# Two-layer encoder trunk in split fp32: the ring of split weights lies 64 bytes further along SBUF

## The chip, the cores and the metric

One core of a Trainium2 chip runs the whole program. The metric is the device time of one execution in microseconds (us), the median of several runs. TensorE (PE, with its weight loads shown apart as PEld), VectorE (DVE), ScalarE (ACT) and GpSimd (POOL) work from SBUF, 128 partitions wide; matmuls write to PSUM; SyncE (SP) issues the DMAs.

## The reference

Two requests of 256 tokens each, 1024 wide, pass through the same two layers. Each layer is a half-step SwiGLU block, a token mixer, another half-step SwiGLU block and a norm:

```python
def swiglu(x, w_gate, w_up, w_down):
    return (jax.nn.silu(x @ w_gate) * (x @ w_up)) @ w_down
...
    for layer in range(DEPTH):
        x = x + 0.5 * swiglu(rms_norm(x, ffn1_norm[layer]), ffn1_w_gate[layer], ffn1_w_up[layer], ffn1_w_down[layer])
        h = rms_norm(x, mix_norm[layer])
...
        x = x + 0.5 * swiglu(rms_norm(x, ffn2_norm[layer]), ffn2_w_gate[layer], ffn2_w_up[layer], ffn2_w_down[layer])
        x = rms_norm(x, final_norm[layer])
```

`D_FF` is 2816. The mixer of layer 0 joins differential attention with neighbourhood attention, that of layer 1 is grouped-query attention with rotary positions; each has one input and one output projection. All is float32.

## The kernel before

**Split operands.** Every float32 operand `a` of a large product is cut into a high part (an fp32r copy) and a low part (the rest, fp32r too), and a product is made of three matmuls: high by high, high by low, low by high. So each piece of weights is loaded by DMA into `raw`, copied by ACT into a tile `wh` (L349, `emit_hi`), and DVE (at times POOL) subtracts to give `wl` (L364, `emit_lo`). `wh` and `wl` are the ring of split weights: 12 tiles of 128 x 512 each (`RING`, L31), 2048 bytes of a partition apiece, reused in turn through the whole program.

**The two SwiGLU blocks of a layer** (`ffn`, L854) take nearly all the time. Gate and up are one product over 22 slices of `D_FF`. For the first two or three slices it is done plainly (`plain`, L957): the weights are the stationary operand and 512 tokens stream past, from the split tokens `xh`, `xl`. For the other slices seven products of blocks stand in for eight (`multiply`, L893, in `product_of`, L906): 128 x 128 weights stationary, 256 tokens streaming, from `xh`, `xl` or from sums of token blocks in `xb`. They go into the banks `ba`, `bb`, `bc`, `bg`. Groups of 4, 6, 6 and 6 slices (`GROUPS`, L22) are followed by the down product (`down`, L1033): weights stationary, 512 columns of the split activations `ah`, `al` streaming. In the last block of all, the last two rows of output go by 256 columns (`down_last`, L1067).

**The mixers.** The input projection (`in_proj_group`, L1248) has it the other way round: tokens `xh`, `xl` are stationary and 256 columns of `wh`, `wl` stream past into `ip`. The output projection (`out_proj`, L1266) is again weights stationary, with 512 columns of `mh`, `ml`, into `op`. Between them lie small matmuls of attention: `sc`, `pt`, `pv`.

**What sets the order.** The order of all instructions is fixed when the program is built: by a planner (`Plan`, L438) and an interleaver (`Interleave`, L1187) that reckon with costs of their own. Neither looks at where a tile lies within its row beyond blocks of 128 elements.

**Where tiles lie.** Pools are laid one behind the other along the partition: `per`, `sm`, `rawp`, `wp`, and then a pool of the stage (`ffn`, `ab` or `cc`). `per` holds the residual `X`, the tokens `xh`, `xl` and the sums `xb`. `sm` holds small tiles of 32 bytes, and one of 256 bytes, `rh` (L810), of which 16 bytes are used. `rawp` holds the two buffers of `raw`, `wp` the ring and the sums of weights `T1` to `T4`. The stage's pool holds `ah`, `al`, `gate`, `dt`, `mh`, `ml` and so on. The tiles of 1 KB and more start, in the program as built, at these bytes of the partition:

| tile | first byte before | past a multiple of 256, before | after |
|---|---|---|---|
| `xh`, `xl` | 33792, 50176 | 0 | 0 |
| `xb` (two) | 69120, 81408 | 0 | 0 |
| `sq`, `sum0`, `X` | 66560, 93696, 17408 | 0 | 0 |
| `sum1` (also `dg`) | 95776 | 32 | 32 |
| `raw` (two) | 100160, 108352 | 64 | 128 |
| ring `wh`, `wl` (24) | 116544 to 163648 | 64 | 128 |
| `T1` to `T4`, `dt`, `gate`, `ah`, `al`, `mh`, `ml` | from 165696 | 64 | 128 |
| `qkh`, `qkl`, `T`, `V` of the first mixer | from 208768 | 128 | 192 |

A weight block within a ring tile starts at a multiple of 512 bytes from the tile's start, a token block at a multiple of 1024, so the table holds for each block as for its tile.

Of the kernel before, what the change touches and what calls it, by code (L numbers as in the profile page):

```python
# [9 lines left out]
F32R = mybir.dt.float32r  # L10
# [5 lines left out]
P = 128  # L16
# [526 lines left out]
def hybrid_trunk_kernel(ctx, tc, x, cst, wgu1, wd1, wgu2, wd2, win_ab, wout_ab, win_c, wout_c, ali, nab, y):  # L543
# [8 lines left out]
    sm = ctx.enter_context(tc.tile_pool(name="sm", bufs=4))  # L552
# [17 lines left out]
    def pvp(name):  # L570
        return clock.alloc(pv_p.tile([P, T], F32, tag="pv", name=name), "pv", BANKS["pv"])

    def small(w, name):
        return sm.tile([P, 8], F32, tag=name, name=name)[:, :w]
# [76 lines left out]
    class Norm:  # L651
# [152 lines left out]
        def spread_steps(self, name, pool, tag):  # L804

            d = {}

            def high():
                d["v"] = getattr(self, name)
                rh = sm.tile([P, 64], F32R, tag="rh", name="rh", bufs=1)[:, :4]  # L810
                A.activation(rh, d["v"], AF.Copy)
                d["h"] = rh.bitcast(F32)

            def low():
                d["l"] = small(4, "rt")
                V.tensor_tensor(d["l"], d["v"], d["h"], ALU.subtract)

            def diagonal(v, tag):
                dg = per.tile([P, 4, P], F32R, tag=tag, name="dg")
                V.tensor_tensor(dg, ident.unsqueeze(1).to_broadcast([P, 4, P]),  # L820
                                d[v].unsqueeze(2).to_broadcast([P, 4, P]), ALU.mult)
                d[tag] = dg

            def spread():
                d["ps"] = pvp("bc")
                for i, tag in enumerate(("sq", "sum1")):
                    PE.matmul(d["ps"], lhsT=ones_r, rhs=d[tag].rearrange("p a b -> p (a b)"), start=(i == 0),
                              stop=(i == 1))

            def copy():  # L830
                self.wide[name] = out = pool.tile([P, T], F32, tag=tag, name=tag, bufs=1)
                V.tensor_copy(out, d["ps"])

            self.wide = getattr(self, "wide", {})
            return [("act", high, [name], ["rh"], 0.1), ("dve", low, [name, "rh"], ["rl"], 0.08),
                    ("dve", lambda: diagonal("h", "sq"), ["rh"], ["sq"], 0.61),
                    ("dve", lambda: diagonal("l", "sum1"), ["rl"], ["sum1"], 0.61),
                    ("pe", spread, ["sq", "sum1"], ["pv"], 0.5), ("dve", copy, ["pv"], [tag], 0.6)]
# [1062 lines left out]
```

## Time and profile before

| | |
|---|---|
| median of 3 runs | 1824.51 us (1820.37 to 1824.85) |
| the profiled execution: its time | 1817.23 us |
| its span, first to last instruction | 1815.5 us |
| mean granted TensorE clock | 0.996 |
| instructions in the span | 31467 |
| DMA | 175.53 MB, mean 97 GB/s |

The profile is of one execution. Busy time is the time in which an engine has at least one instruction under way. A matmul's record is longer than the time until the next one starts, since matmuls are pipelined. So a stretch of W us, in which x records are seen, has one matmul started every (W + length of one record) / x; this is called the pitch below. A name such as `ba<-xh,wh` gives the tile that is written and those that are read; buffer numbers are left out. Nearly all instructions carry line 151, the helper that records them, so tiles tell them apart, not lines.

### The profile page before, as it was taken

To read this page: it belongs to the slowest core of one execution; us is meant where nothing else is said; L and a number is where in the kernel's file an instruction comes from. 1 tells how busy PE (TensorE), PEld (TensorE's weight loads), DVE (VectorE), ACT (ScalarE), POOL (GpSimd) and SP (SyncE) were. 2 spreads that over 40 slices of the span, in tenths; PEclk is the share of its full clock that TensorE was granted. 3 is DMA by queue.
4 is the path that set the end of the run, shared out by engine and by line. 5 is a ranking of instruction groups with operands and counts; after the bars stand their busy time and mean duration, and the time that the engine had idled before them with its cause. 6 is when DMAs were issued, how large, how long until landed. Compare 5 with 4: busy or idle time off the path is not lost.

```text
span 1815.5 us, 31467 instructions
## 1 busy us (share of the span) xinstructions
PE 1772.1 (98%) x12428; PEld 1616.8 (89%) x12428; DVE 1517.2 (84%) x2849; ACT 959.4 (53%) x1975; POOL 155.9 (9%) x110
## 2 busy tenths in 40 slices
PE   8999999999899999999999999999998999999997
PEld 7998989898798889898978999999986788989896
DVE  8998979757886899898899989898777788989895
ACT  7463636445555646363665545455355664636362
POOL 0000000043431000000000000000344100000000
PEclk9999999999999999999999999999999999999999
DMA  4332323222212134141412232323121113324231
GB/s 153 119 129 91 119 91 120 105 94 71 82 71 94 47 117 141 69 145 67 142 67 93 96 117 97 113 99 132 53 71 47 68 39 128 129 82 136 74 117 47
DMA packets 31700, 175.53 MB, mean 97 GB/s; under 512 B 3392, under 2 KB 5696, under 8 KB 17088
## 3 DMA queue, kind: packets, MB, share of 16 engines
q1 hardware_dynamic: 31552, 173.52, 27.9%
q8 instruction: 97, 1.59, 0.4%
q14 instruction: 51, 0.42, 0.1%
HBM read 171.41 MB, written 2.10 MB: 96 GB/s over the span
## 4 chain that ended last, share of the span: by engine, by line
PE 78%; DVE 12%; ACT 5%; issue 2%; DMA 1%; POOL 1%; SPq 0%; POOLq 0%; ACTq 0%; DVEq 0%
PE ba L151 30%; PE bb L151 13%; PE bc L151 12%; PE bg L151 11%; PE ip L151 6%; PE op L151 4%; DVE wl L151 2%; ACT att L151 2%; DVE att L151 1%; PE pv L151 1%; DVE X L151 1%; DVE nm L151 1%; DVE dt L151 1%; DMA raw<-wd 1%; DVE xl L151 1%
## 5 line engine op out<-in xcount | busy, mean ns | idle before, releaser
L151 ACT ACTIVATE wh<-raw 128x512 fp32r<-128x512 f32 x553 | 337.8, 626 | 218.5 <-PE ba L151 63.2
L151 DVE TENSOR_TENSOR wl<-raw,wh 128x512 fp32r<-128x512 f32 x516 | 371.1, 727 | 59.4 <-ACT wh L151 53.5
L151 ACT ACTIVATE wh<-T 128x512 fp32r<-128x512 f32 x316 | 197.0, 629 | 262.5 <-PE ba L151 138.7
L151 PE MATMUL bc<-xb,wh 128*128 128x256 f32 x1264 | 225.7, 278 | 3.7 <-DVE us L151 3.2
L151 DVE TENSOR_TENSOR wl<-T,wh 128x512 fp32r<-128x512 f32 x316 | 215.2, 685 | 15.9 <-ACT wh L151 13.9
L151 PE MATMUL ba<-xh,wh 128*128 128x256 f32 (+1 forms) x704 | 204.7, 291 | 3.8 <-ACT wh L151 3.8
L151 PE MATMUL ba<-al,wh 128*128 128x512 f32 (+1 forms) x534 | 206.0, 386 | 0.0
L151 PE MATMUL ba<-ah,wh 128*128 128x512 f32 (+1 forms) x534 | 205.9, 386 | 0.0
L151 PE MATMUL ba<-ah,wl 128*128 128x512 f32 (+1 forms) x534 | 205.9, 386 | 0.0
L151 PE MATMUL ba<-xh,wl 128*128 128x256 f32 (+1 forms) x704 | 204.6, 291 | 0.0
L151 PE MATMUL ba<-xl,wh 128*128 128x256 f32 (+1 forms) x704 | 204.4, 290 | 0.0
L151 PEld LDWEIGHTS bc<-xb,wh 128*128 128x128 f32 x1264 | 191.0, 188 | 5.1 <-DVE us L151 3.6
L151 PE MATMUL bc<-xb,wl 128*128 128x256 f32 x632 | 175.2, 277 | 0.0
L151 PE MATMUL ip<-wh,xh 128*128 128x256 f32 x576 | 166.0, 288 | 0.0
L151 PE MATMUL ip<-wh,xl 128*128 128x256 f32 x576 | 160.7, 279 | 0.6 <-DVE xl L151 0.6
L151 PE MATMUL ip<-wl,xh 128*128 128x256 f32 x576 | 160.5, 279 | 0.0
L151 PEld LDWEIGHTS ba<-xh,wh 128*128 128x128 f32 x704 | 133.1, 189 | 7.8 <-ACT wh L151 4.0
L151 PEld LDWEIGHTS ba<-xh,wl 128*128 128x128 f32 x704 | 132.8, 189 | 3.9 <-DVE wl L151 0.5
L151 PEld LDWEIGHTS ba<-xl,wh 128*128 128x128 f32 x704 | 132.7, 189 | 3.4
L151 PEld LDWEIGHTS bc<-xb,wl 128*128 128x128 f32 x632 | 118.8, 188 | 0.0
L151 PEld LDWEIGHTS ba<-ah,wl 128*128 128x128 f32 x534 | 100.3, 188 | 20.1
L151 PEld LDWEIGHTS ba<-al,wh 128*128 128x128 f32 x534 | 100.3, 188 | 19.8 <-DVE al L151 0.2
(204 smaller groups left out, 4364.0 us busy)
## 6 DMA issues: line engine op xcount, KB each, us to landing
raw<-wgu SPq DMA_DIRECT2D x87, 1024.0 KB, 4.7
raw<-wd SPq DMA_DIRECT2D x48, 768.0 KB, 4.1
raw<-win_ab SPq DMA_DIRECT2D x12, 1024.0 KB, 4.7
raw<-wd SPq DMA_DIRECT2D x16, 512.0 KB, 3.6
raw<-win_c SPq DMA_DIRECT2D x6, 1024.0 KB, 4.8
raw<-wout_ab SPq DMA_DIRECT2D x4, 1024.0 KB, 4.8
raw<-wout_c SPq DMA_DIRECT2D x4, 1024.0 KB, 4.7
X<-x SPq DMA_DIRECT2D x8, 256.0 KB, 5.1
```

Source lines behind the costliest of these rows:

```text
L151: return f(*args, **kw)
```

## The change

The tile `rh` is made 80 elements wide in place of 64, 320 bytes in place of 256. Its used part stays four elements. What lies in front of it stays where it is; what lies behind it in the partition, the rest of `sm`, `raw`, the ring and the pools of the stages, starts 64 bytes later. On each of the five engines the program has the same instructions in the same order as before, on the same tiles.

```diff
             def high():
                 d["v"] = getattr(self, name)
-                rh = sm.tile([P, 64], F32R, tag="rh", name="rh", bufs=1)[:, :4]
+                rh = sm.tile([P, 80], F32R, tag="rh", name="rh", bufs=1)[:, :4]
                 A.activation(rh, d["v"], AF.Copy)
                 d["h"] = rh.bitcast(F32)
```

So the pairs that a matmul reads, streaming operand and stationary operand, lie like this (bytes past a multiple of 256):

| matmuls | streaming, before / after | stationary, before / after | distance, before / after |
|---|---|---|---|
| gate and up of the SwiGLU blocks | 0 / 0 | 64 / 128 | 64 / 128 |
| input projections `ip` | 64 / 128 | 0 / 0 | 64 / 128 |
| down products, output projections `op` | 64 / 128 | 64 / 128 | 0 / 0 |

## The prediction

> **What bounds the kernel now.** I began with the page: the busy line, the granted clock and the chain that ended last.
>
> ```profile
> span 1815.5 us, 31467 instructions
> PE 1772.1 (98%) x12428; PEld 1616.8 (89%) x12428; DVE 1517.2 (84%) x2849; ACT 959.4 (53%) x1975; POOL 155.9 (9%) x110
> PEclk9999999999999999999999999999999999999999
> PE 78%; DVE 12%; ACT 5%; issue 2%; DMA 1%; POOL 1%; SPq 0%; POOLq 0%; ACTq 0%; DVEq 0%
> ```
>
> TensorE streams for 98% of the span, at a steady clock, and holds 78% of the chain. It stands still for 1815.5 - 1772.1 = 43 us in all. The table of waits shows the side that keeps pace:
>
> ```profile
> ACT wh L151 <- PE ba L151: 201.8, 153, 4.5
> ```
>
> ACT waits 202 us, in 153 waits, for TensorE to give a ring tile back. The ring is filled ahead; what a matmul costs on TensorE comes out in the total.
>
> The change touches only where operands lie, so the question is whether a matmul's pitch depends on that. I read steady stretches one after the other, by windows of the PE records. Columns: window, width, busy time with the number of records, granted clock, DMA share, GB/s.
>
> ```profile
> 172.00:200.00 28.00, 28.00 (x249) 1.00 0.33 112
> 206.00:228.00 22.00, 22.00 (x189) 1.00 0.50 159
> 871.00:904.00 33.00, 33.00 (x282) 1.00 0.43 141
> 358.00:385.00 27.00, 27.00 (x232) 1.00 0.40 140
> 600.00:608.00 8.00, 8.00 (x36) 1.00 0.00 0
> 232.00:260.00 28.00, 28.00 (x125) 1.00 0.19 71
> ```
>
> The groups of matmuls by line, in those windows (rows one to five: 172 to 200, 206 to 228, 358 to 385, 600 to 608, 232 to 260) and in one at 430.8 to 434 (the last row), give what ran and the mean record:
>
> ```profile
> L151 PE MATMUL bc<-xb,wh 128*128 128x256 f32 x48 | 8.5, 276 | 0.0
> ...
> L151 PE MATMUL bc<-xb,wh 128*128 128x256 f32 x38 | 6.9, 281 | 0.0
> ...
> L151 PE MATMUL ip<-wh,xh 128*128 128x256 f32 x78 | 21.8, 280 | 0.0
> ...
> L151 PE MATMUL ba<-xh,wl 128*128 128x512 f32 x6 | 2.4, 396 | 0.0
> ...
> L151 PE MATMUL ba<-ah,wl 128*128 128x512 f32 x30 | 11.7, 389 | 0.0
> ...
> L151 PE MATMUL ip<-wh,xh 128*128 128x256 f32 x10 | 2.8, 276 | 0.0
> ```
>
> With pitch = (width + record) / records:
>
> - gate and up, 256 columns, operands 64 bytes apart: 28.276 / 249 = 113.6 ns in one stretch, 22.281 / 189 = 117.9 ns in another (33.281 / 282 = 118.0 in a third);
> - `ip`, 256 columns, also 64 apart but the other way round: 27.280 / 232 = 117.6 ns, and in the short window records of 276 again. It has the same two gaits;
> - plain gate and up, 512 columns, 64 apart: 8.396 / 36 = 233.2 ns;
> - down, 512 columns, 0 apart: 28.389 / 125 = 227.1 ns.
>
> The clock is 1.00 in every row, and the fast gait and the slow one have a DMA share of 0.33 and 0.43 to 0.50. The last rows of output are 256 columns at distance 0. Their timeline (start, length):
>
> ```profile
> 1793.42 0.28 PE L151 MATMUL ba<-ah,wh 128*128 128x256 f32 x1
> ...
> 1797.98 0.28 PE L151 MATMUL bg<-ah,wl 128*128 128x256 f32 x1
> ```
>
> With the rows between, these make 38 steps in 4.56 us: 120.0 ns, slower than either gait. The same group by line shows the longer record:
>
> ```profile
> L151 PE MATMUL ba<-ah,wl 128*128 128x256 f32 x12 | 3.4, 283 | 0.0
> ```
>
> So at 256 columns the pitch is 113.6 or 117.9 at distance 64, and 120.0 at distance 0. At 512 columns the order is reversed, 233.2 against 227.1. That these differences belong to the distance is an inference: the products compared differ in it, but they differ in their tiles and their place in the program too.
>
> A reason why distance could matter is that every matmul has a weight load of its own, whose record is longer than the pitch, so that some weights are always being read while a stream is:
>
> ```profile
> L151 PEld LDWEIGHTS bc<-xb,wh 128*128 128x128 f32 x1264 | 191.0, 188 | 5.1 <-DVE us L151 3.6
> ```
>
> **The change part by part.** No instruction, wait, transfer or byte is added. Moved tiles of DVE and ACT first. These rows are operations on tiles at 0 and 32 bytes, at 64, at 64, and at 0:
>
> ```profile
> L151 DVE TENSOR_TENSOR sum<-sum,sq 128x512 f32<-128x512 f32 x49 | 33.6, 686 | 8.5 <-ACT sq L151 8.4
> L151 DVE TENSOR_TENSOR wl<-T,wh 128x512 fp32r<-128x512 f32 x316 | 215.2, 685 | 15.9 <-ACT wh L151 13.9
> L151 ACT ACTIVATE wh<-T 128x512 fp32r<-128x512 f32 x316 | 197.0, 629 | 262.5 <-PE ba L151 138.7 <-DVE T L151 62.4 <-PE bc L151 25.6
> L151 ACT ACTIVATE sq<-X 128x512 f32<-128x512 f32 x47 | 29.4, 625 | 35.0 <-DVE X L151 34.7 <-DMA X<-x 0.2
> ```
>
> 686 against 685 ns and 629 against 625: these engines don't see the place. I cost them at nothing; were it those 4 ns on each of ACT's 1975 instructions, that is 8 us on an engine idle for half the span. Down and `op` stay at distance 0 and cost nothing either.
>
> What is left is TensorE's three kinds of pairs that go from 64 apart to 128 apart. Groups over the whole run (of gate and up the first, one between and the last of 13 groups, 1264 + 5 x 632 + 7 x 316 = 6636 matmuls; of `ip` all; of plain, the first and the last of six):
>
> ```profile
> L151 PE MATMUL bc<-xb,wh 128*128 128x256 f32 x1264 | 225.7, 278 | 3.7 <-DVE us L151 3.2 <-ACT bc L151 0.5
> ...
> L151 PE MATMUL ba<-xh,wl 128*128 128x256 f32 x632 | 175.1, 277 | 0.0
> ...
> L151 PE MATMUL bg<-xh,wl 128*128 128x256 f32 x316 | 87.5, 277 | 0.0
> L151 PE MATMUL ip<-wh,xh 128*128 128x256 f32 x576 | 166.0, 288 | 0.0
> L151 PE MATMUL ip<-wh,xl 128*128 128x256 f32 x576 | 160.7, 279 | 0.6 <-DVE xl L151 0.6
> L151 PE MATMUL ip<-wl,xh 128*128 128x256 f32 x576 | 160.5, 279 | 0.0
> L151 PE MATMUL ba<-xh,wh 128*128 128x512 f32 x72 | 29.6, 411 | 3.8 <-ACT wh L151 3.8
> L151 PE MATMUL bb<-xl,wh 128*128 128x512 f32 x72 | 28.4, 395 | 0.0
> ```
>
> The record tells the gait: 276 is 113.6 and 281 is 117.9, or 0.86 ns of pitch for each ns of record. Gate and up, at 277, run at 113.6 + 0.86 = 114.5 ns in the mean. `ip`, at 279, runs at 113.6 + 3 x 0.86 = 116.2 (the 288 of the first group holds long records behind waits). Plain runs at 233.2, its longer means being starts.
>
> No row has two operands 128 apart in a 256-column split product, so this price is bounded by the rows near it. The best is all in the fast gait, 113.6; the worst seen is that of distance 0, 120.0. Which is nearer? Gate and up stream from 0 over weights at 64; `ip` streams from 64 over weights at 0. The distance is +64 in one and -64 in the other, and both show the same two gaits (113.6 and 117.9; 276 records and 117.6). If only the distance modulo some period counts, and +64 and -64 are alike, the simplest period that makes them alike is 128, and then 128 apart is the same as 0 apart. I take 120.0, in both kinds, and for plain the 227.1 of distance 0:
>
> - gate and up: 6636 x (120.0 - 114.5) = +36.5 us;
> - `ip`: 1728 x (120.0 - 116.2) = +6.6 us;
> - plain: 432 x (227.1 - 233.2) = -2.6 us;
> - in all +40.5 us.
>
> All of it lies on TensorE, which has no cover for it but its own waits. Of those, gate and up show 3.7 + 3.8 us in front of the rows above; a slower stream lets DVE and ACT catch up there, so up to 7 us may come back. The profiled execution took 1817.2 us; 1817.2 + 40.5 = 1857.7, down to 1850 with that. The profiled time lies 7 us under the median of 1824.5. If other executions merely spend more of it in the slow gait, their sum ends at the same place, since at distance 0 there is but one pitch; if the 7 us come from elsewhere, it is 1865. I say **1858**.
>
> The Trainium skill bears on this with a rule that speaks against any effect; it stands beside the rival B.
>
> **The rivals.**
>
> *A, the forecast:* distance 128 acts as distance 0. For it: the symmetry of +64 and -64, and the fact that distance 0 has one pitch, not two. Against it: that symmetry would hold for any longer period too if only the size of the distance counted.
>
> *C, faster:* the period is 256 bytes or more, distance 0 is the worst, 64 is a partly cured case that at times falls into the slow gait, and 128 is far enough never to. All 256-column products run at 113.6, and plain at 227.1. Gain: 6636 x 0.9 = 6.0, 1728 x 2.6 = 4.5, 432 x 6.1 = 2.6, in all 13.1 us, giving 1817.2 - 13.1 = 1804 by the profiled execution and 1811 by the median. It decides once the pitch of gate and up falls below today's 114.5, that is once their records fall under 277. For it: 120.0, then 113.6 to 117.9, is a course that improves with distance. Against it: one step of 64 is all that the profile has, and at 512 columns 64 is worse than 0.
>
> *D, slower, but half the way:* 128 leaves the two gaits as they are and the stream always falls into the slow one. 6636 x (117.9 - 114.5) + 1728 x (117.9 - 116.2) = 22.6 + 2.9 = 25.5 us, giving 1843. For it: the gaits last through whole stretches (33 us in one row), so something at a stretch's start selects them, and the place may. Against it: gate and up prefer the fast one now.
>
> *B, nothing:* weights and stream are read apart, so their distance is of no account, and the pitches come from something else: the down product's own tiles, what went before a stretch. The sum is then 0, and the time stays at the median, 1824.5. It covers too that only 0 is special and any other distance is like 64. Against it stand the rows of one shape at one clock: 113.6, 117.9 and 120.0. The Trainium skill states this rule: by "TensorE: Matmul & The Clock Gate", "Step-by-step: what each phase is for", the PE has two independent read ports in SBUF, and loading the next weights takes no read bandwidth from the running matmul. By that rule no distance could change a pitch; the trace, with its 120.0 against 113.6 ns, does not agree with it cleanly, though it doesn't show the cause.
>
> That the change does nothing to the places is no rival: the byte table of the built program has every ring tile 64 further on, and `xh`, `xl`, `xb` where they were.
>
> **How the numbers follow.** A 0.42, D 0.10, B 0.20, C 0.28. The symmetry is the only argument that picks a value for 128, so A leads, but it is an argument from two pairs, hence less than half. About 0.3% of 1824.5, 5.5 us, is what a measurement of this kernel can tell from no change. A (+33 to +41) and D (+25) are slower by more, C (-13) is faster by more, B is within it: faster 0.28, same 0.20, slower 0.52. The likeliest case's own range is 1848 to 1866. To leave out no more than 2 in 10 the range must take in C, whose lower end is 1804; so it is 1804 to 1866.
>
> **What the changed profile would show.** Under A: records of 283 in every group of gate and up and of `ip`, a pitch of 120.0 in any steady window of them, no stretch of 276; plain at 389 like down; down, `op` and the last rows as now; PE busy up by some 40 us; more of ACT's waiting on TensorE, DVE and ACT durations unchanged within 1%. Under C: 276 everywhere and no 281. Under D: 281 everywhere. Under B: both gaits as now and the tail alone at 120.0. I am wrong in the step on the period if records stay at 281 or less; wrong in the step on cover if records are 283 and the time is under 1848; and wrong from the ground up if down or the tail, whose distance doesn't change, change their pitch, since then the place itself counts and not the distance.

## The result and the profile after

The changed kernel takes 1846.90 us in the median of 4 runs (1845.66 to 1851.23), the kernel before 1822.44 us (1816.20 to 1824.85, 4 runs). The ratio is 1.0144, with a 95% interval of 1.0127 to 1.0161: 24 us slower by the medians, 26 us by the means (1847.7 and 1821.5, which give that ratio). Every run of the changed kernel is slower than every run of the kernel before. The profiled execution took 1846.73 us, its span 1845.0 us against 1815.5. Here the difference is 29.5 us, because the execution of the kernel before that was profiled, at 1817.23 us, lies under that kernel's median.

The page of the changed kernel shows the busy line, the clock and the chain:

```profile
span 1845.0 us, 31467 instructions
PE 1802.7 (98%) x12428; PEld 1648.7 (89%) x12428; DVE 1525.8 (83%) x2849; ACT 967.2 (52%) x1975; POOL 155.7 (8%) x110
PEclk9999999999999999999999999999999999999999
PE 76%; DVE 14%; ACT 5%; issue 2%; DMA 1%; POOL 1%; SPq 0%; POOLq 0%; DVEq 0%; ACTq 0%
```

The program is the same by its count of instructions, and so is the clock. TensorE is busy for 30.6 us more (1772.1 to 1802.7), which is the whole growth of the span, 29.5 us. Its idle time is what it was, 1845.0 - 1802.7 = 42 us. The groups of matmuls by line, over the whole run:

```profile
L151 PE MATMUL bc<-xb,wh 128*128 128x256 f32 x1264 | 232.1, 281 | 3.0 <-DVE us L151 3.0
...
L151 PE MATMUL ba<-xh,wl 128*128 128x256 f32 x632 | 177.8, 281 | 0.0
...
L151 PE MATMUL ip<-wl,xh 128*128 128x256 f32 x576 | 162.5, 282 | 0.0
...
L151 PE MATMUL bb<-xl,wh 128*128 128x512 f32 x72 | 28.4, 395 | 0.0
...
L151 PE MATMUL ba<-ah,wl 128*128 128x256 f32 x18 | 5.1, 283 | 0.0
```

Records of gate and up go from 277 or 278 to 281, those of `ip` from 279 to 282. Plain keeps its 395, the last rows their 283. Gate and up don't reach the 283 of the forecast; the mean of `ip` has long records behind waits in it, and in the steady window below all its groups show 281. Three steady windows of the PE records (gate and up twice, then `ip`) give the pitch:

```profile
206.00:228.00 22.00, 22.00 (x188) 1.00 0.43 139
871.00:904.00 33.00, 33.00 (x281) 1.00 0.26 89
365.00:388.00 23.00, 23.00 (x197) 1.00 0.36 121
```

22.281 / 188 = 118.5 ns, 33.281 / 281 = 118.4, 23.281 / 197 = 118.2; one record more or less in such a window is half a ns. The first two have DMA shares of 0.43 and 0.26 and the same pitch, so it doesn't follow the transfers. These are the values of the slow gait to within the window's grain, and the record of 281 is that gait's too. But it isn't that gait. The times from one start to the next, in the order of the trace, in ns, for gate and up at 900 us, in the kernel before (slow gait), after, and below it the fast gait of before at 180 us:

```
before, 900 us:  118 118 117 119 117 118 118 118 117 118 118 117 119 117 118
after,  900 us:  115 118 121 120 119 115 118 122 120 119 115 117 122 120 119
before, 180 us:  113 114 113 113 114 113 113 114 113 113 114 113 113 114 113
```

After the change five matmuls make a cycle, 115, 118, 122, 120 and 119 ns, though the tiles repeat in threes (`xh,wh`, `xl,wh`, `xh,wl`), and the same five-step cycle stands in `ip`, where tokens and weights have changed sides. In gate and up it holds from one end of the program to the other.

In what follows "mean pitch" is the mean of these start-to-start times over a whole run, of the 256-column split products, those of 126 ns or more (a wait, or the first after one) left out: 6617 of gate and up before and 6632 after; 1618 and 1608 of `ip`. It went from 114.30 to 118.67 ns in gate and up, from 116.91 to 118.65 in `ip`.

### The profile page after: what moved, and what is told of

Its sections match the earlier page's. It is cut to its first block, busy times and chain, and to the rows that moved or that the text cites. A ratio compares the mean times of both kernels' runs of the same rounds, so it can differ in the third digit from the quotient of the medians.

```text
span 1845.0 us, 31467 instructions
## 1 busy us (share of the span) xinstructions
PE 1802.7 (98%) x12428; PEld 1648.7 (89%) x12428; DVE 1525.8 (83%) x2849; ACT 967.2 (52%) x1975; POOL 155.7 (8%) x110
## 4 chain that ended last, share of the span: by engine, by line
PE 76%; DVE 14%; ACT 5%; issue 2%; DMA 1%; POOL 1%; SPq 0%; POOLq 0%; DVEq 0%; ACTq 0%
PE ba L151 28%; PE bb L151 12%; PE bc L151 12%; PE bg L151 11%; PE ip L151 6%; PE op L151 4%; DVE wl L151 3%; ACT att L151 2%; DVE X L151 1%; PE pv L151 1%; DVE att L151 1%; DMA raw<-wd 1%; DVE nm L151 1%; DVE xl L151 1%; DVE room L151 1%
## 5 line engine op out<-in xcount | busy, mean ns | idle before, releaser
L151 PE MATMUL bc<-xb,wh 128*128 128x256 f32 x1264 | 232.1, 281 | 3.0 <-DVE us L151 3.0
```

The lines of the kernel that those rows point to most:

```text
L151: return f(*args, **kw)
```

## The experiments

The main theory is that the **distance** between the two places that a matmul reads, weights minus stream modulo 256 bytes, sets the pitch. The main rival is **place**: where the ring itself lies. All ten kernels compute the full reference, and differ from the kernel before in the padding alone. A pad in front of `X` (wider `cs`) moves tokens and ring together; a narrower or wider `rh` moves the ring alone.

**e1: the ring as in the change, the tokens moved along.**

```diff
-    cs = per.tile([P, NPER + 24], F32, name="cs")
+    cs = per.tile([P, NPER + 40], F32, name="cs")
-    comb = cs[:, NPER + 16:]
+    comb = cs[:, NPER + 16:NPER + 24]
```

> The ring lies at 128 past a multiple of 256 as in the change, but xh, xl, xb and all else in their pool lie 64 further on too, so that every distance is that of the kernel before (64, 64 and 0). Theory 'distance' (the pitch follows from streaming place minus stationary place): both gaits of before are back, gate and up with records of 276 to 281 and a mean near 277, ratio 1.000 within 0.004. Rival 'place' (the ring's own place counts): as after the change, mean record 281 in gate and up, no long stretch of 276, ratio 1.014.

Measured: 1820.30 us, ratio 1.0010 (0.9997 to 1.0023). Groups and one window of this kernel:

```profile
L151 PE MATMUL bc<-xb,wh 128*128 128x256 f32 x1264 | 225.7, 278 | 3.2 <-DVE us L151 2.5 <-ACT bc L151 0.6
...
L151 PE MATMUL ip<-wl,xh 128*128 128x256 f32 x576 | 161.5, 280 | 0.0
```

```profile
172.00:200.00 28.00, 28.00 (x249) 1.00 0.33 114
```

278 and 249 records: the fast gait is back in that window to the record, with the ring where the change put it. Mean pitch 114.29 in gate and up and 116.91 in `ip`. Place falls.

**e2: the ring as before, the tokens moved to 192.**

```diff
-    cs = per.tile([P, NPER + 24], F32, name="cs")
+    cs = per.tile([P, NPER + 72], F32, name="cs")
-    comb = cs[:, NPER + 16:]
+    comb = cs[:, NPER + 16:NPER + 24]
-                rh = sm.tile([P, 64], F32R, tag="rh", name="rh", bufs=1)[:, :4]
+                rh = sm.tile([P, 16], F32R, tag="rh", name="rh", bufs=1)[:, :4]
```

> The mirror of e1: the ring stays at 64 as before, and xh, xl, xb go to 192, so that gate and up and the input projections have a distance of 128. 'Distance': as after the change, starts of 115, 118, 122, 120, 119 ns in turn, mean 118.7, records of 281 in gate and up and 282 in the input projections, ratio 1.014. 'Place' of the ring: as before, ratio 1.000.

Measured: 1847.54 us, ratio 1.0153 (1.0131 to 1.0175).

```profile
L151 PE MATMUL bc<-xb,wh 128*128 128x256 f32 x1264 | 232.1, 282 | 1.9 <-DVE us L151 1.9
...
L151 PE MATMUL ip<-wl,xh 128*128 128x256 f32 x576 | 162.6, 282 | 0.0
```

The five-step cycle is there, mean pitch 118.67 and 118.68, with the ring in its old place. e1 and e2 together: the price of the change is that of the pair, and of neither side alone.

**e3: the ring at 128, but another 128.** Here `rh` is `[P, 16]`.

> The tile rh of 16 elements: the ring at 128 past a multiple of 512, where the change has 384 past a multiple of 512. Distance 128 modulo 256 in both. If the period is 256 or less: as the change, ratio 1.014, mean start to start 118.7 ns. If the period is 512, the distance is +128 where it is -128 in the change for gate and up, and the other way round for the input projections; the two kinds agree after the change, so a period of 512 with size alone gives 1.014 too, and only a difference between the two signs would show as another pitch.

Measured: 1845.62 us, ratio 1.0144 (1.0121 to 1.0166), mean pitch 118.66 and 118.61. 128 and 384 past a multiple of 512 are alike. A period of 512 that looks at the size alone isn't excluded by this, as the expectation says; e6 and e7 below bear on that.

**e4: the ring at 0, all distances 0.** `rh` is `[P, 48]`.

> The tile rh of 48 elements: the ring at 0, all distances 0. 'Distance': the 120.0 ns of the last rows holds for every 256-column product: records of 283 in gate and up and in the input projections, plain at 389 and 227 ns; 6636 x (120.0 - 114.5) + 1728 x (120.0 - 116.5) - 432 x 6.1 = 36.5 + 6.0 - 2.6 = +40 us, ratio 1.022. Rival: the 120.0 belonged to the down product's own tiles or to the end of the program; then gate and up show another pitch, and the ratio lies between 1.000 and 1.015.

Measured: 1855.91 us, ratio 1.0195 (1.0171 to 1.0219).

```profile
L151 PE MATMUL bc<-xb,wh 128*128 128x256 f32 x1264 | 234.5, 283 | 1.8 <-DVE us L151 1.8
...
L151 PE MATMUL ip<-wl,xh 128*128 128x256 f32 x576 | 162.8, 283 | 0.0
```

The records are the 283 that the last rows have, and 6582 of the 6630 steps of gate and up are 120 ns. This is what the prediction wanted from the change: the price of distance 0 was read rightly from the tail of before, but the change doesn't produce distance 0. Plain, at 512 columns, fell as well, from a mean start-to-start time of 233.2 ns to 228.1 (steps over 245 ns left out), so there too it is the distance that counts.

**e5 to e8: other places in steps of 32.** `rh` is `[P, 56]`, `[P, 72]`, `[P, 88]` and `[P, 32]`; the ring at 32, 96, 160 and 192.

> The tile rh of 56 elements: the ring at 32, distance 32 in gate and up and in the input projections, 0 elsewhere. Theory 'blocks' (the two readers meet in blocks of 64 bytes, only the whole number of blocks between them counts): 32 acts as 0 or as 64, so a pitch of 120.0 (ratio 1.020) or the two gaits of before (1.000). Rival 'fine' (every byte of distance counts): a pitch of its own, between 113.3 and 120.0, ratio between 0.995 and 1.020.

Measured: 1841.41 us, ratio 1.0124 (1.0109 to 1.0139). Mean pitch 118.33 in gate and up, 116.89 in `ip`. 32 is neither as 0 nor as 64: blocks of 64 bytes fall. The two kinds differ, which a rule by size alone doesn't give.

> The tile rh of 72 elements: the ring at 96, distance 96. 'Blocks': as 64 (two gaits, ratio 1.000) or as 128 (118.7 ns, ratio 1.014). 'Fine': a pitch of its own; if 64 is the best distance of all, above 114.3 ns in the mean; if the fast gait at 64 is only the edge of a better stretch, 113.3 ns everywhere, 6617 x 1.0 + 1618 x 3.6 = 12 us less, ratio 0.993.

Measured: 1848.97 us, ratio 1.0161 (1.0144 to 1.0178). 118.62 and 119.85 ns: a pitch of its own, and no better stretch beyond 64.

> The tile rh of 88 elements: the ring at 160, distance 160 or -96 modulo 256. If only the size of the distance modulo 256 counts, as +64 and -64 suggest: the same mean pitch as at 96, in gate and up and in the input projections alike. If the sign counts off the multiples of 64: gate and up here have the pitch that the input projections have at 96, and the other way round.

Measured: 1854.39 us, ratio 1.0193 (1.0178 to 1.0209). 120.00 and 118.10 ns. The groups of e6, then of e7:

```profile
L151 PE MATMUL ba<-xh,wl 128*128 128x256 f32 x632 | 177.4, 281 | 0.0
...
L151 PE MATMUL ip<-wl,xh 128*128 128x256 f32 x576 | 162.9, 283 | 0.0
```

```profile
L151 PE MATMUL ba<-xh,wl 128*128 128x256 f32 x632 | 178.8, 283 | 0.0
...
L151 PE MATMUL ip<-wl,xh 128*128 128x256 f32 x576 | 161.9, 281 | 0.0
```

281 and 283 become 283 and 281. What gate and up have at 96, `ip` has nearly at 160, and the other way round: the sign counts, and a period of 256 fits. That a longer one isn't needed rests on three columns of the table below: modulo 512, the distances of gate and up and of `ip` are 352 and 96 in the column of 96, 416 and 160 in that of 160, 384 and 128 in that of 128, and the pitches agree within 0.6 ns. A period of 512 by size alone is out, since in e6 gate and up at 352 (which is -160) and `ip` at 160 differ, 118.62 against 119.85. In the other columns both kinds have the same distance modulo 512, so there 256 is not tested.

> The tile rh of 32 elements: the ring at 192, distance -64 modulo 256 for gate and up and +64 for the input projections, which is before with the two kinds exchanged. Period 256 with size alone: both gaits as before, mean of gate and up within 0.7 ns of 114.3, ratio 1.000 within 0.004. If the sign picks the gait (gate and up prefer the fast one now, the input projections the slow one): gate and up mostly at 117.8, 6617 x 2.5 = +17 us, and the input projections mostly at 113.3, 1618 x -2.5 = -4 us, ratio 1.007.

(The expectation multiplies by 2.5 ns where 117.8 - 114.3 is 3.5 and 116.9 - 113.3 is 3.6; with these it is 23 - 6 = 17 us and a ratio of 1.010.) Measured: 1837.64 us, ratio 1.0102 (1.0086 to 1.0117). Groups and two windows, gate and up and then `ip`:

```profile
L151 PE MATMUL ba<-xh,wl 128*128 128x256 f32 x632 | 176.3, 279 | 0.0
L151 PE MATMUL ip<-wl,xh 128*128 128x256 f32 x576 | 160.5, 279 | 0.0
```

```profile
875.00:900.00 25.00, 25.00 (x215) 1.00 0.30 106
365.00:385.00 20.00, 20.00 (x179) 1.00 0.41 138
```

25.28 / 215 = 117.6 ns and 20.28 / 179 = 113.3. Gate and up run at 117.75 in the mean, in the slow gait from end to end; `ip` at 115.62, now in the fast gait for about half of its steps against a fifth before. So +64 and -64 are not alike either: both know the two gaits, but -64 of weights minus stream falls mostly into the slow one. The records differ too: in the slow gait they are 281 ns at +64 (gate and up before, `ip` here) and 279 to 280 at -64 (`ip` before, gate and up here), so a record stands for a gait only at one distance.

**e9: what lies behind the ring moved, the ring not.**

```diff
         lo = self.clock.alloc(self.pool.tile([P, 512], F32R, tag="wl", name=f"wl{k}", bufs=RING), "wl", RING)
+        if k == 0:
+            self.pool.tile([P, 16], F32, tag="pad", name="pad", bufs=1)
```

> The other half of the change alone: the ring stays at 64, and what lies behind it (ah, al, gate, mh, ml and the other tiles of the stages) goes 64 further. The change moved both and left the down products at distance 0; here the down and output products have weights minus stream = -64. Theory 'signed distance modulo 256': gate and up and the input projections as before (114.3 and 116.9 ns in the mean), no change of DVE and ACT durations, and the 512-column down products take the 229.4 ns that the plain products have at weights minus stream = 192 (e8): 2438 x (229.4 - 227.1) = +5.6 us, ratio 1.003; by the 233.2 ns of distance +64 it is +15 us, ratio 1.008. The last rows of 256 columns at 117.8 in place of 120.0. Rival 'moved tiles cost by themselves' : DVE or ACT durations grow by over 1%. Rival 'only equal distances of 256 columns count': no change at all, 1.000.

Measured: 1827.25 us, ratio 1.0042 (1.0029 to 1.0054).

```profile
L151 PE MATMUL ba<-ah,wl 128*128 128x512 f32 x516 | 202.3, 392 | 0.0
...
L151 PE MATMUL ip<-wl,xh 128*128 128x256 f32 x576 | 161.2, 280 | 0.0
...
L151 PE MATMUL ba<-ah,wl 128*128 128x256 f32 x18 | 5.0, 279 | 0.0
```

The group of down shown goes from 389 to 392. The mean pitch of down and `op` (starts over 245 ns left out) goes from 227.03 to 229.07, which is 2429 x 2.04 = 5.0 us. The last rows fall from 283 to 279, and their mean start-to-start time from 119.8 to 117.7 ns, which is what gate and up have at 192 in e8: a third kind of matmul follows the distance. Gate and up and `ip` were to stay at 114.3 and 116.9 and have 114.04 and 117.19; their place is the old one, but the share of steps in the fast gait isn't quite the same (84% against 79% in gate and up). The conversions keep their times: the page has 627 ns for `wh<-raw` and 727 for `wl<-raw,wh` (before 626 and 727). So moving the tiles of these operations of DVE and ACT is free, and the part behind the ring costs something only when the ring does *not* go with it.

**e10: the ring at 224.** `rh` is `[P, 40]`.

> The tile rh of 40 elements: the ring at 224, the one step of 32 that is left. Weights minus stream is 224 for gate and up, 32 for the input projections, which is e5 with the kinds exchanged. 'Signed distance modulo 256': gate and up at 116.9 ns (what the input projections have in e5), the input projections at 118.3; 6617 x (116.9 - 114.3) + 1618 x (118.3 - 116.9) = +17 + 2 = +19 us, ratio 1.0107. If only the size counts: gate and up at 118.3 as in e5, +27 us, ratio 1.0145.

Measured: 1834.61 us, ratio 1.0084 (1.0070 to 1.0098).

```profile
L151 PE MATMUL ba<-xh,wl 128*128 128x256 f32 x632 | 176.4, 279 | 0.0
...
L151 PE MATMUL ip<-wl,xh 128*128 128x256 f32 x576 | 162.3, 282 | 0.0
```

Mean pitch 116.67 and 118.29 ns, where the exchange with e5 asked for 116.9 and 118.3. The ratio ends a little under the 1.0107 forecast, which lies outside its interval; the rival's 1.0145 is further out.

All the mean pitches at 256 columns, by weights minus stream modulo 256:

| weights minus stream | 0 | 32 | 64 | 96 | 128 | 160 | 192 | 224 |
|---|---|---|---|---|---|---|---|---|
| gate and up, ns | 119.99 (e4) | 118.33 (e5) | 114.30 (before) | 118.62 (e6) | 118.67 (after) | 120.00 (e7) | 117.75 (e8) | 116.67 (e10) |
| `ip`, ns | 119.67 (e4) | 118.29 (e10) | 115.62 (e8) | 118.10 (e7) | 118.65 (after) | 119.85 (e6) | 116.91 (before) | 116.89 (e5) |

The columns agree within 0.6 ns but for 64 and 192, where there are two gaits to choose from. The kernel before has its dominant kind in the best column; no measured place of the ring beats it. Giving `ip` the column of 64 too would be worth some 1618 x (116.91 - 115.62) = 2 us by e8's mean, too little to be told from no change, and wasn't tried. Places off the steps of 32 weren't tried.

## Why the prediction was right, and where it failed

**The time: right in part by luck.** 1846.9 us lies in the range of 1804 to 1866, but just under the 1848 to 1866 of the likeliest case, whose 1858 is 11 us too high; the range reaches below 1848 because rival C was let in. That the change makes the kernel slower was right, but it was drawn from a period that is wrong. No row of before held the price at 128, and any price above the 114.5 that gate and up had would have given the same direction.

**TensorE's pitch and nothing else: right.** DVE, ACT, down and the last rows kept their durations within 1 or 2 ns. In the changed kernel the conversions, 685 and 629 ns before, are

```profile
L151 ACT ACTIVATE wh<-T 128x512 fp32r<-128x512 f32 x316 | 198.3, 630 | 280.2 <-PE ba L151 143.0
...
L151 DVE TENSOR_TENSOR wl<-T,wh 128x512 fp32r<-128x512 f32 x316 | 215.7, 686 | 23.4 <-ACT wh L151 20.3
```

and the growth of PE's busy time (30.6 us) is that of the span (29.5).

**That the pair's distance sets the pitch: right.** The prediction called it an inference; e1 and e2 show it. The eight columns range from 114.3 to 120.0 ns. That it is the weight load which the stream meets is still only argued: the runs show the dependence on the two places, not who stops whom. The Trainium skill ("TensorE: Matmul & The Clock Gate", "Step-by-step: what each phase is for") says that loading the next weights takes no read bandwidth from the running matmul. If that were all, the columns would be equal; here the measurement decides that the pitch does depend on where the two operands lie, though no run shows by what way.

**The step that failed: "the simplest period that makes them alike is 128, and then 128 apart is the same as 0 apart".** Both halves are wrong. +64 and -64 looked alike because each shows two gaits, but their means already differed (114.3 and 116.9; the prediction's own figures were 114.5 and 116.2), and so did the slow gait's records (281 in gate and up, 279 to 280 in `ip`); e8 shows that the sign matters. And 128 is not as 0: it has a cycle of its own, at 118.67 ns against 119.99 in e4, that no row of before contained. The sign that the prediction named for this error, records of 281 or less, came in gate and up. The price of 120.0 itself was right for distance 0 (e4, 119.99).

**The terms.** Summed from start to start with their waits: gate and up went from 764.4 to 791.0 us, +26.6 where +36.5 stood; `ip` from 219.1 to 222.7, +3.6 where +6.6 stood; plain from 103.9 to 103.4, -0.5 where -2.6 stood (its pitch stayed at 232.6 ns and didn't fall to the 228.1 of distance 0 in e4). That is 29.7 us, against 40.5, and the rest nearly cancels. At distance 0 itself, in e4, the same sums grow by 34.4 and 3.9 and fall by 2.3: 36.0 us. So of the 10.8 us that the forecast has too much, 6.3 belong to the period; the other 4.5 lie mostly in the cover (below) and in `ip`, which was charged 3.8 ns for each of 1728 matmuls where e4 shows 2.8 for the 1618 that no wait stands beside. Its 116.2 came from reading a record of 279 as a mixture of the two gaits, where it was mostly the slow gait at -64.

**The cover: a small part of it.** The idle time in front of the two groups that the prediction names went from 3.7 + 3.8 to 3.0 + 3.5 us: 1 us came back of the 7 allowed for. By start-to-start times it is a little more: the 256-column matmuls of gate and up took 5.9 us beyond their mean pitch before and 3.5 after, so 2.4 us came back (3.4 us in e4). And as forecast, ACT waits longer for TensorE, shown by the table of waits of the changed kernel (before: 201.8 us):

```profile
ACT wh L151 <- PE ba L151: 210.1, 157, 4.1
```

**The rivals.** D came nearest by its number (1843) for the wrong reason: not the slow gait always, which is what e8 shows in gate and up, but a third pattern of about the same mean. The mean record of 281 stands for both in gate and up, so the sign named for D didn't tell them apart; the single starts did. C failed by its premise that the far point is the best. B is out for 128, as moving one operand changes the pitch (e2) and moving both doesn't (e1).

**What isn't settled** is why there are two gaits at 64 and 192, what picks one at a restart, and why 128 has five steps.

## What to carry to other kernels

Where TensorE is the bound and each matmul loads its own weights, look at where the weights and the streaming tile lie modulo 256 bytes: a pad of 64 bytes, moved by any small tile in front, was worth 1.4% here, and 2% in the other direction (e4). Compare pitches of the same shape in steady stretches, and read single start-to-start times before calling two patterns the same. A symmetry seen in two means is no period; measure one more point before extrapolating from it.

## What the runs showed of the hardware

- At 256 fp32r columns the start-to-start time depends on the signed distance of weights and stream modulo 256 bytes (measured in steps of 32), at a granted clock of 1.00: from 113.3 ns in the fast gait at 64 to 120.0 at 0 and 160.
- The pattern doesn't follow the tiles: at 128 it repeats every five matmuls, where the tiles repeat every three.
- At 64 and at 192 two patterns are possible, 113.3 and 117.8 ns; one is kept from one wait to the next, up to 504 matmuls in the trace of before.
- At 512 columns the effect is smaller in proportion and its order another: 226.9 ns (down before) and 228.1 (plain in e4) at 0, 229.0 (down in e9) and 229.4 (plain in e8) at 192, 232.6 at 128 and 233.2 at 64 (plain after and before).
